# The order of two adaLN tiles on VectorE in the ramp, and a mean taken out by TensorE in the last pieces of a residual block

## The chip, the cores and the metric

One Trainium2 chip, of which one core is used. A core has TensorE (PE in the profile; PEld is its weight loads), VectorE (DVE), ScalarE (ACT), GpSimd (POOL) and SyncE (SP), which issues the loads and stores. TensorE reads on-chip memory and writes only the accumulation banks (PSUM, eight banks of 128x512 fp32 here); VectorE and ScalarE read both, GpSimd only the on-chip memory. The metric is the device time of one execution in microseconds, lower is better.

## The reference

A block of three sublayers over x of 256 x 2048 (fp32), conditioned on a vector c. From c come nine vectors of 2048, `silu(c) @ w_ada + b_ada`: a shift, a scale and a gate for each sublayer.

```python
mod = (jax.nn.silu(c) @ w_ada[l] + b_ada[l]).reshape(B, N_SUBLAYERS, 3, D_MODEL)
shift, scale, gate = mod[:, :, 0], mod[:, :, 1], mod[:, :, 2]

def modulate(h, s):
    return _layer_norm(h) * (1.0 + scale[:, s, None, :]) + shift[:, s, None, :]

y = _swiglu(modulate(x, 0), ffn1_w13[l], ffn1_w2[l])
x = _layer_norm(ALPHA * x + FFN_WEIGHT * gate[:, 0, None, :] * y, ln_g[l, 0], ln_b[l, 0])
...
y = _swiglu(modulate(x, 2), ffn2_w13[l], ffn2_w2[l])
x = _layer_norm(ALPHA * x + FFN_WEIGHT * gate[:, 2, None, :] * y, ln_g[l, 2], ln_b[l, 2])
```

The middle sublayer, left out here, is a mixer of mLSTM heads and a gated recurrence. The change touches the start of the first feed-forward sublayer (FFN1) and the layer norm that ends the last one (FFN2).

## The kernel before, in words

**Numbers.** Products are made of fp32 numbers split in two parts: `hi`, a cast by ScalarE, and `lo`, the rest, by VectorE (`split`, lines 90 to 100). A product then has three matmuls: hi x hi, hi x lo, lo x hi. In a few places both operands stay fp32 and one "whole" matmul does it; the profile shows such a matmul as two records.

**The ramp** (`ramp`, lines 682 to 824) is the start of FFN1. The shift and scale come as adaLN tiles: tile `ada<i>` is 128x2048 weights, and VectorE reduces it against the row of silu(c) (`ada_tile`, line 181) to one column of shift or of scale. Only then can 128 rows of the modulated input u be made, so the ramp goes through the 16 blocks of 128 in stages of 3, 4, 4 and 5 (`STAGES`). In each stage TensorE multiplies the blocks made so far by the weight tiles `rra<n>` (`hra`, `lra` once split), and the partial sums are kept on chip. At the end of a stage (line 781) the u of the next one is made: `ada_until` reduces the adaLN tiles that are still missing, and `modulate` (line 223) lets TensorE transpose two blocks into a bank, ScalarE apply scale and shift to each (line 236) and cast both to the high part (line 239), and VectorE make the low part (line 240). In stage 0 the blocks 3 and 4 are made by a first `modulate` (tile `u0_3`), blocks 5 and 6 by a second (tile `u0_5`). adaLN tiles ada12 and ada13 are the shift and the scale of block 6. The first products of stage 1 are whole ones with the unsplit tile 9 (line 803), the next use tile 10.

**The order.** While `wide[0]` holds, the operations on VectorE and SyncE are recorded through a helper (line 122) that keeps them in program order; all these have L122 in the profile. Elsewhere a scheduler places them. Every engine works off its own queue in order, and the raw tiles live in a few buffers that are used again in turn.

**The end** (`closing`, line 880, and `boundary`, line 330, with `following` None). The output is 2 halves of 128 rows (t = 0, 1) by 4 pieces of 512 columns (n = 0 to 3). Pieces n = 0, 1, 2 get their residual from `residual` (line 309), which also gathers statistics; only n = 3 is left for `boundary`. `products(1)` makes the last product `tl` of rows 128 to 255. `take` adds it to x and gathers statistics, and `norm` aggregates them to mean and variance (`mvp`), lets GpSimd make the reciprocal root `rsp` in two operations, and runs VectorE over the four pieces twice: first (x - mean) * ln_g (line 376), then times rsp plus ln_b (line 386). Each finished piece is stored at once (line 387). x keeps the result in place.

Of the kernel before, what the change touches and what calls it, by code (L numbers as in the profile page):

```python
# [11 lines left out]
F32 = mybir.dt.float32  # L12
# [4 lines left out]
P = 128  # L17
# [30 lines left out]
def block_kernel(ctx: ExitStack, tc: tile.TileContext, a: dict, out: bass.AP):  # L48
# [145 lines left out]
    def ada_until(s, j, kt):  # L194

        while any(key == (s, j, kt) for _, key in todo):
            ada_tile(V if wide[0] else nc.vector)
# [132 lines left out]
    def boundary(s, ps, hls, order, mm, sts, following, gated=False):  # L330
# [19 lines left out]
        def products(t):  # L350
            for n in order[t]:
                if (t, n) not in ps:
                    ps[t, n] = bank(f"tl{s}{t}{n}")
                mm(ps[t, n], t, n)

        def take(t, n):

# [7 lines left out]
            V.bn_stats(sts[t][:, n, :], x[:, t, cs[n]])  # L365
            yield

        def norm(t):

            mv = sm.tile([P, 2], F32, tag="mv", name=f"mvp{s}{t}")  # L370
            V.bn_aggr(mv, sts[t].rearrange("p a b -> p (a b)"))
            r = rstd_in_order(mv[:, 1:2], f"p{s}{t}")

            sq = sums[t] = sm.tile([P, 2, 4], F32, tag="sq", bufs=2, name=f"sq{s}{t}")
            for c in cs:
                V.scalar_tensor_tensor(x[:, t, c], x[:, t, c], mv[:, 0:1], g[:, c], op0=ALU.subtract, op1=ALU.mult)
                yield
            for n, c in enumerate(cs):
                if following:
                    V.scalar_tensor_tensor(x[:, t, c], x[:, t, c], r, b[:, c], op0=ALU.mult, op1=ALU.add,  # L380
                                           accum_out=sq[:, 0, n:n + 1])
                    junk = sm.tile([P, 512], F32, tag="gy" if t else "u", bufs=2, name=f"junk{s}{t}{n}")
                    A.activation(junk, x[:, t, c], AF.Square, bias=sbs, scale=D ** -0.5,
                                 accum_out=sq[:, 1, n:n + 1])
                else:
                    V.scalar_tensor_tensor(x[:, t, c], x[:, t, c], r, b[:, c], op0=ALU.mult, op1=ALU.add)
                    nc.sync.dma_start(out[t * P:(t + 1) * P, c], x[:, t, c])
                yield
            if following:
                tot = tots[t] = sm.tile([P, 4], F32, tag="tot", bufs=2, name=f"tot{s}{t}")  # L390
                V.tensor_reduce(tot[:, 0:2], sq, op=ALU.add, axis=mybir.AxisListType.X)

                V.tensor_scalar(tot[:, 2:3], tot[:, 0:1], 1.0 / D, sb, op0=ALU.mult, op1=ALU.add)
                V.scalar_tensor_tensor(tot[:, 3:4], tot[:, 2:3], tot[:, 2:3], tot[:, 1:2], op0=ALU.mult,
                                       op1=ALU.subtract)
                r = rstd_in_order(tot[:, 3:4], f"n{s}{t}", -1.0)
                nm_ = sm.tile([P, 2], F32, tag="nb", name=f"nbn{s}{t}")
                A.activation(nm_[:, 0:1], tot[:, 2:3], AF.Identity, bias=sb, scale=-1.0)
                A.activation(nm_[:, 1:2], nm_[:, 0:1], AF.Copy, scale=r)
                mrb[t] = nm_[:, 0:1], r, nm_[:, 1:2]  # L400
                yield
# [55 lines left out]
        def takes(t, ns):  # L457
            for n in ns:
                yield from take(t, n)

        def run(steps, m=100):
            for _ in range(m):
                if next(steps, steps) is steps:
                    return

        mrb, sums, tots = {}, {}, {}
        products(0)
        for k in ready:
            fw[k] = split(fw[k], nc.scalar, V)
        run(takes(0, order[0]))  # L470
        products(1)
        if not following:
            run(norm(0))
            run(takes(1, order[1]))
            run(norm(1))
            return

        A.activation(b, b, AF.Identity, accum_out=sb)
# [136 lines left out]
    def ffn(s, w13, w2, start, following=None):  # L615
# [66 lines left out]
        def ramp(ns):  # L682
# [5 lines left out]
            for st, k in enumerate(STAGES):  # L688
# [89 lines left out]
                for b in range(RAMP // 4):  # L778
                    for p in range(2):

                        if b == RAMP // 4 - 1 and p == (k > 2) and not last:
                            k1 = k0 + k
                            tile_of(3 * k - 1)
                            wide[0] = st < len(STAGES) - 2
                            ahead = load(a["w13_r"][n_w + 3 * k], f"ra{n_w + 3 * k}")
                            unsplit = [] if first else None
                            if not first:
                                ahead = split(ahead, nc.scalar, V if wide[0] else nc.vector)
                            ada_until(0, 1, k1 + 1)
                            modulate(0, ns, k1, 2, vec=V if wide[0] else nc.vector, kept=unsplit)  # L790
                            ada_until(0, 1, k1 + STAGES[st + 1] - 1)
                            made = modulate(0, ns, k1 + 2, STAGES[st + 1] - 2, vec=V if wide[0] else nc.vector, kept=unsplit)
                        if (b, p) in held:
                            pss = held[b, p]
                        else:
                            pss = banks(b, p)
                            with ExitStack() as stack:
                                for m in made if b < 2 else ():
                                    stack.enter_context(tc.issue_after(m.ins))
                                if st == 1 and (b, p) == (0, 0):  # L800
                                    for j in range(k):
                                        for t in range(NT):
                                            end = nc.tensor.matmul(
                                                pss[t], unsplit[j][:, t * P:(t + 1) * P],
                                                ahead[0][:, j * 512:(j + 1) * 512], start=j == 0, stop=j == k - 1)
                                else:
                                    end = products(b, p, pss, 0, k)
                                for i in range(k if first else 0, 0 if last else min(3 * k, ((2 * b + p + 3) * k + 3) // 4)):
                                    tile_of(i)
                        if b != KEPT:  # L810
                            for t in range(NT):
                                if first:
                                    A.copy(part[b, p][t], pss[t])
                                else:
                                    (nc.vector if last else V).tensor_add(part[b, p][t], part[b, p][t], pss[t])
                        if first and b < 2 and p:
                            tile_of(4 + b)
                        turn_one(end)
                    if last and b < 4:
                        g, v = (kept if b == KEPT else {p: part[b, p] for p in range(2)}).values()  # L820
                        for t in range(NT):
                            swiglu(b, t, g[t], v[t])
# [57 lines left out]
        def closing(gi):  # L880

            kgs = [(kg, hts[kg // 2], kg % 2 * 4) for kg in (2 * gi - 2, 2 * gi - 1, 2 * gi)]
            pss, hls = {}, {}

            def gated(k, into=None):

                tile = load(w2[kgs[k][0] * 4 + 3], f"w2{s}l{k}", into)
                for c in range(0, D, 512):
                    nc.vector.tensor_mul(tile[0][:, c:c + 512], tile[0][:, c:c + 512], gate[:, 1536:])
                hls[k] = split(tile, nc.scalar, nc.vector)  # L890

            for i, (n, k) in enumerate(((0, 0), (0, 1), (1, 0), (0, 2), (1, 1), (1, 2), (2, 0), (2, 1), (2, 2))):
                kg, h, k0 = kgs[k]
                if not k:
                    pss[n] = [bank(f"tl{s}{t}{n}") for t in range(NT)]
                end = mov_w(pss[n], load_w(w2[kg * 4 + n], f"w2{s}_{kg}_{n}"), *h, k0, not k, k == 2)
                if i:
                    turn_one(end)

                if i in (2, 5):  # L900
                    gated(i // 2, half(i // 5))
                if k == 2:
                    for t in range(NT):
                        residual(s, t, n, pss[n][t], sts, nc.vector)
            credit[:] = 0.0, 0.0
            fine[0] = True
            gated(0)

            def last(ps, t, n):
                for i, (_, h, k0) in enumerate(kgs):  # L910
                    mov_t(ps, hls[i], *h, k0, t, i == 0, i == 2)

            boundary(s, {}, hls, ((3,), (3,)), last, sts, None, True)

# [491 lines left out]
```

## Time and profile before

| | us |
|---|---|
| median of 3 runs | 1898.51 (1898.49 to 1898.91) |
| the profiled execution, its own time | 1898.66 |
| its span, first to last instruction | 1896.9 |
| TensorE busy | 1878.0 |
| VectorE busy | 1412.4 |
| ScalarE busy | 830.8 |
| granted TensorE clock, mean of the span | 0.998 of full |

The page lists the busy time of each engine, the span in 40 slices, the DMA queues, a chain of work followed back from the last instruction, and the costliest groups. Times within the execution are counted from its first instruction. In a row of the timeline stand the start, the length, the engine, the line, the operation, what it writes and reads (buffer numbers left out), its shape, the count, and in brackets the idle time of the engine before it and what ended it. A row of groups ends in count | busy us, mean ns | idle before it and its releasers. A row of waits has the total, the number and the longest.

### The profile page before, as it was taken

Reading aid. Unit: us, or ns where it says so; the run is one execution under the profiler, and the core shown is the slowest. Engines: PE = TensorE matmul, PEld = TensorE weight load, DVE = VectorE, ACT = ScalarE, POOL = GpSimd, SP = SyncE. Lnnn points to the kernel's source line nnn. Section 1 sums busy time; section 2 is a strip of 40 time slices with the busy share of each in tenths; the row PEclk is TensorE's granted clock in tenths of the full one; section 3 lists DMA queues with packets and bytes.
Section 4 is the critical chain, followed back from the end, with each engine's and each line's share of the span. In section 5 each row is a group of like instructions: output and inputs, shape, how many; then the busy total and the mean of one; then the engine's idle time right before and its main releaser. Section 6 shows DMA issues by size and latency. Waiting matters only on the chain.

```text
span 1896.9 us, 21238 instructions
## 1 busy us (share of the span) xinstructions
PE 1878.0 (99%) x8583; PEld 1542.9 (81%) x8583; DVE 1412.4 (74%) x1372; ACT 830.8 (44%) x788; POOL 39.3 (2%) x65
## 2 busy tenths in 40 slices
PE   9999999999999999999999999999999999999997
PEld 6788888888888888788888887888888888888886
DVE  6899998887887977799987877556555644545676
ACT  4443444534334335756643357343434334343340
POOL 0000000000000000000000121000000000000000
PEclk9999999999999999999999999999999999999999
DMA  9989889999999886477787563666666655555562
GB/s 379 404 349 362 321 314 354 353 346 347 353 359 356 333 327 247 174 278 273 275 320 270 218 245 132 242 255 247 241 258 240 230 192 197 182 198 205 195 222 89
DMA packets 74498, 515.87 MB, mean 272 GB/s; under 512 B 8688, under 2 KB 8864, under 8 KB 13472
## 3 DMA queue, kind: packets, MB, share of 16 engines
q1 hardware_dynamic: 72144, 507.54, 71.0%
q10 hardware_dynamic: 1728, 3.80, 0.6%
q0 software_dynamic: 528, 3.17, 0.4%
q8 instruction: 67, 1.10, 0.2%
q14 instruction: 31, 0.25, 0.0%
HBM read 512.36 MB, written 2.12 MB: 271 GB/s over the span
## 4 chain that ended last, share of the span: by engine, by line
PE 93%; DVE 3%; ACT 2%; DMA 1%; issue 1%; POOL 0%; DVEq 0%; SPq 0%; ACTq 0%
PE py L272 6%; PE py L271 6%; PE py L273 6%; PE fg L272 6%; PE fg L271 6%; PE fg L273 6%; PE fv L271 6%; PE fv L272 6%; PE fv L273 6%; PE pj L260 5%; PE pj L262 3%; PE tl L271 2%; PE tl L272 2%; PE tl L273 2%; PE rv L720 2%; PE rv L721 2%
## 5 line engine op out<-in xcount | busy, mean ns | idle before, releaser
L191 DVE CUSTOM_DVE_ANT_0 ada<-ada,scb,badac 128x2048 f32<-128x2048 f32 x110 | 258.0, 2346 | 12.7 <-DMA ada<-in_w_ada 12.6
L99 DVE TENSOR_TENSOR lw<-rw,hw 128x2048 fp32r<-128x2048 f32 x81 | 185.3, 2290 | 92.9 <-ACT hw L97 92.9
L97 ACT CAST hw<-rw 128x2048 fp32r<-128x2048 f32 x81 | 155.0, 1914 | 220.3 <-PE py L273 78.6
L99 DVE TENSOR_TENSOR lfv<-rfv,hfv 128x2048 fp32r<-128x2048 f32 x60 | 137.5, 2292 | 132.5 <-ACT hfv L97 132.4
L99 DVE TENSOR_TENSOR lfg<-rfg,hfg 128x2048 fp32r<-128x2048 f32 x60 | 137.5, 2291 | 90.6 <-ACT hfg L97 90.6
L272 PE MATMUL py<-lw,hth 128*128 128x512 f32 x512 | 199.4, 389 | 0.1
L273 PE MATMUL py<-hw,htl 128*128 128x512 f32 x512 | 199.4, 389 | 0.0
L97 ACT CAST hfg<-rfg 128x2048 fp32r<-128x2048 f32 x60 | 114.9, 1915 | 191.4 <-PE fv L273 57.5
L271 PE MATMUL py<-hw,hth 128*128 128x512 f32 x512 | 197.7, 392 | 0.0
L272 PE MATMUL fg<-lfg,u 128*128 128x512 f32 x480 | 187.0, 389 | 0.1
L273 PE MATMUL fg<-hfg,u 128*128 128x512 f32 x480 | 187.0, 389 | 0.0
L272 PE MATMUL fv<-lfv,u 128*128 128x512 f32 x480 | 186.8, 389 | 0.0
L273 PE MATMUL fv<-hfv,u 128*128 128x512 f32 x480 | 186.7, 389 | 0.0
L97 ACT CAST hfv<-rfv 128x2048 fp32r<-128x2048 f32 x60 | 114.7, 1912 | 164.1 <-PE fg L273 91.7
L271 PE MATMUL fg<-hfg,u 128*128 128x512 f32 x480 | 185.0, 392 | 0.0
L271 PE MATMUL fv<-hfv,u 128*128 128x512 f32 x480 | 183.5, 389 | 0.0
L260 PE MATMUL pj<-u,hs 128*128 128x512 f32 x512 | 122.5, 391 | 0.0
L97 ACT CAST hra<-rra 128x2048 fp32r<-128x2048 f32 x38 | 72.6, 1916 | 102.5 <-DMA rra<-in_w_r 47.7
L272 PEld LDWEIGHTS py<-lw,hth 128*128 128x128 f32 x512 | 96.2, 188 | 20.4 <-DVE lw L99 0.9
L273 PEld LDWEIGHTS py<-hw,htl 128*128 128x128 f32 x512 | 96.1, 188 | 20.2
L271 PEld LDWEIGHTS py<-hw,hth 128*128 128x128 f32 x512 | 95.9, 188 | 19.3
L260 PEld LDWEIGHTS pj<-u,hs 128*128 128x128 f32 x512 | 94.3, 188 | 18.4
(464 smaller groups left out, 3545.9 us busy)
## 6 DMA issues: line engine op xcount, KB each, us to landing
ada<-in_w_ada SPq DMA_DIRECT2D x138, 1024.0 KB, 6.2
rw<-in_w SPq DMA_DIRECT2D x81, 1024.0 KB, 5.0
rfg<-in_w SPq DMA_DIRECT2D x60, 1024.0 KB, 4.9
rfv<-in_w SPq DMA_DIRECT2D x60, 1024.0 KB, 4.8
rra<-in_w_r SPq DMA_DIRECT2D x45, 1024.0 KB, 7.2
rs<-in_w_s SPq DMA_DIRECT2D x32, 1024.0 KB, 5.0
rwo<-in_w_out SPq DMA_DIRECT2D x16, 1024.0 KB, 4.8
rv<-in_w_vo SPq DMA_DIRECT2D x8, 1024.0 KB, 4.8
```

The lines of the kernel that those rows point to most:

```text
L97: act.copy(cut(hi, w), like(raw[:, w], hi))
L99: low.tensor_sub(cut(lo, w), like(raw[:, w], lo), cut(hi, w).bitcast(F32))
L191: vec.tensor_tensor_reduce(raw[:, c], raw[:, c], scb[:, c], 1.0, base, ALU.mult, ALU.add, to)
L260: nc.tensor.matmul(ps, hi[:, k * P:(k + 1) * P], both(k), start=k == 0, stop=False)
L262: nc.tensor.matmul(ps[:, 0:S], lo[:, k * P:(k + 1) * P], uh[:, k, :], start=False, stop=k == KT - 1)
L271: nc.tensor.matmul(o, acth[:, k0 + j, tk], cut(hi, w), start=first and j == 0, stop=False)
L272: nc.tensor.matmul(o, acth[:, k0 + j, tk], cut(lo, w), start=False, stop=False)
L273: end = nc.tensor.matmul(o, actl[:, k0 + j, tk], cut(hi, w), start=False, stop=last and j == 3)
L720: pe.matmul(pss[t], uh[:, k0 + j, tk], hi[:, w], start=go, stop=False)
L721: pe.matmul(pss[t], uh[:, k0 + j, tk], lo[:, w], start=False, stop=False)
```

## The change

Two edits.

In the ramp the second `ada_until` (up to the last block of the next stage) takes the place of the first and comes ahead of the first `modulate`. VectorE's queue at the end of stage 0, as a difference (- before, + now; `ada12` and `ada13` are the reductions of block 6, `u0_3` the low part of blocks 3 and 4, `u0_5` of blocks 5 and 6):

```order
-L122 TENSOR_TENSOR u2_114<-u0_3_505,u2_114 128x2x256
-L122 ISA ada12_510,adac_116<-ada12_510,scb_80,badac_115 128x2048
-L122 ISA adac_116 128x1
-L122 ISA ada13_513,adac_116<-ada13_513,scb_80,badac_115 128x2048
-L122 ISA adac_116 128x1
+L122 ISA ada12_500,adac_116<-ada12_500,scb_80,badac_115 128x2048
+L122 ISA adac_116 128x1
+L122 ISA ada13_503,adac_116<-ada13_503,scb_80,badac_115 128x2048
+L122 ISA adac_116 128x1
+L122 TENSOR_TENSOR u2_114<-u0_3_511,u2_114 128x2x256
 L122 TENSOR_TENSOR u2_114<-u0_5_521,u2_114 128x2x256
```

The low part of `u0_3` moved behind both reductions, next to the low part of `u0_5`. In the ramp nothing else differs: the queues of TensorE, ScalarE and SyncE hold the same instructions in the same order, and at the ends of stages 1 and 2 VectorE's does too, since no adaLN tile is missing there.

At the end, pieces n = 0 and 1 of rows 128 to 255 (`early`) take another way. After their statistics VectorE multiplies them by ln_g; TensorE, behind the last product, copies each into a bank with a whole product by the identity (start) and adds -mean * ln_g to it by a product of ln_g with a diagonal of -mean (stop), which ScalarE makes in two operations. The last pass over these two reads the bank (`tz`). The pieces 2 and 3 go as before, and now first. VectorE's last rows before, from the last product's sum on:

```order
L122 TENSOR_TENSOR x<-x,tl_12778 128x512
L122 BN_STATS sts_8511<-x 128x6
L122 BN_AGGR mvp_12836<-sts_8511 128x2
L122 SCALAR_TENSOR_TENSOR x<-x,mvp_12836,ln_g_12735 128x512 x4
L122 SCALAR_TENSOR_TENSOR x<-x,rsp_12840,ln_b_12737 128x512 x4
```

And VectorE's last rows now:

```order
L122 TENSOR_TENSOR x<-x,tl_12782 128x512
L122 BN_STATS sts_8511<-x 128x6
L122 BN_AGGR mvp_12842<-sts_8511 128x2
L122 SCALAR_TENSOR_TENSOR x<-x,mvp_12842,ln_g_12735 128x512 x2
L122 SCALAR_TENSOR_TENSOR x<-x,rsp_12846,ln_b_12737 128x512 x2
L122 SCALAR_TENSOR_TENSOR x<-tz_12739,rsp_12846,ln_b_12737 128x512
L122 SCALAR_TENSOR_TENSOR x<-tz_12740,rsp_12846,ln_b_12737 128x512
```

Two passes with the mean are gone, and two of the passes with the root read banks. The two products with ln_g stand further ahead on VectorE, between the last split of a weight tile (line 99) and the residual of piece 2 (line 313). TensorE's last rows now, of which the four with `tz` are new (`dm` is the diagonal):

```order
L273 MATMUL tl_12782<-u_114,htl_12382 128x512
L122 MATMUL tz_12739<-x,ident 128x512
L122 MATMUL tz_12740<-x,ident 128x512
L122 MATMUL tz_12739<-ln_g_12735,dm_12851 128x512
L122 MATMUL tz_12740<-ln_g_12735,dm_12851 128x512
```

All four stand behind the last product of the kernel. The diff, cut to what does this:

```diff
@@ products, in boundary
-                mm(ps[t, n], t, n)
+                end = mm(ps[t, n], t, n)
+            return end
@@ norm, in boundary
-        def norm(t):
+        def norm(t, early={}):
...
-            for c in cs:
+            if early:
+                nm_ = sm.tile([P, 2], F32, tag="nb", name=f"nbn{s}{t}")
+                A.mul(nm_[:, 0:1], mv[:, 0:1], -1.0)
+                diag = sm.tile([P, 512], F32, tag="gy", bufs=2, name=f"dm{s}{t}")[:, 0:P]
+                A.activation(diag, ident, AF.Copy, scale=nm_[:, 0:1])
+                for n in early:
+                    T.matmul(early[n], diag, g[:, cs[n]], start=False, stop=True)
+            for n, c in enumerate(cs):
+                if n in early:
+                    continue
                 V.scalar_tensor_tensor(x[:, t, c], x[:, t, c], mv[:, 0:1], g[:, c], op0=ALU.subtract, op1=ALU.mult)
                 yield
-            for n, c in enumerate(cs):
+            for n in sorted(range(4), key=lambda n: n in early):
+                c = cs[n]
...
-                    V.scalar_tensor_tensor(x[:, t, c], x[:, t, c], r, b[:, c], op0=ALU.mult, op1=ALU.add)
+                    V.scalar_tensor_tensor(x[:, t, c], early.get(n, x[:, t, c]), r, b[:, c], op0=ALU.mult, op1=ALU.add)
@@ boundary
+        if not following:
+            early = {n: bank(f"tz{s}{n}") for n in (0, 1)}
+            for n in early:
+                V.tensor_mul(x[:, 1, cs[n]], x[:, 1, cs[n]], g[:, cs[n]])
         products(0)
...
-        products(1)
+        end = products(1)
         if not following:
             run(norm(0))
+            with tc.issue_after(end.ins):
+                for n in early:
+                    T.matmul(early[n], ident, x[:, 1, cs[n]], start=True, stop=False)
             run(takes(1, order[1]))
-            run(norm(1))
+            run(norm(1, early))
             return
@@ ramp
-                            ada_until(0, 1, k1 + 1)
+                            ada_until(0, 1, k1 + STAGES[st + 1] - 1)
                             modulate(0, ns, k1, 2, vec=V if wide[0] else nc.vector, kept=unsplit)
-                            ada_until(0, 1, k1 + STAGES[st + 1] - 1)
                             made = modulate(0, ns, k1 + 2, STAGES[st + 1] - 2, vec=V if wide[0] else nc.vector, kept=unsplit)
```

In `closing`, the function `last` now returns the last matmul, for the order above.

More of the change, by code (lines that the diff above doesn't have):

```diff
@@ L910, in last @@
                 for i, (_, h, k0) in enumerate(kgs):
-                    mov_t(ps, hls[i], *h, k0, t, i == 0, i == 2)
+                    end = mov_t(ps, hls[i], *h, k0, t, i == 0, i == 2)
+                return end
             boundary(s, {}, hls, ((3,), (3,)), last, sts, None, True)
```

## The prediction

> **What bounds the kernel now.** First the page's busy shares and its chain of work that ended last.
>
> ```profile
> PE 1878.0 (99%) x8583; PEld 1542.9 (81%) x8583; DVE 1412.4 (74%) x1372; ACT 830.8 (44%) x788; POOL 39.3 (2%) x65
> PE 93%; DVE 3%; ACT 2%; DMA 1%; issue 1%; POOL 0%; DVEq 0%; SPq 0%; ACTq 0%
> ```
>
> TensorE (PE) is busy for 99% of the span and carries 93% of the chain, so time can be gained only where TensorE stands still, or after its last product. The view of waits, for TensorE alone, says where it stands still; these are the two rows that touch the change.
>
> ```profile
> PE rv L721 <- DVE lra L122: 0.7, 1, 0.7
> PE rg L803 <- ACT u L236: 0.4, 1, 0.4
> ```
>
> Both are one-time waits at the turn from ramp stage 0 to stage 1. The chain of waits from 70 to 84 us (start, length, what) says what they hang on.
>
> ```profile
> 71.94 2.35 DVE ada L122
> 74.29 2.27 DVE ada L122
> 76.60 0.57 ACT u L236
> ...
> 78.79 1.81 ACT hra L97
> 80.62 2.30 DVE lra L122
> 82.97 0.50 PE rv L721
> ```
>
> Two adaLN reductions (ada12, ada13) on VectorE release the last u of the stage, then ScalarE casts it, copies two banks and splits weight tile 10, VectorE makes that tile's low part, and TensorE goes on. The reductions start only at 71.94, and the timeline of VectorE shows why:
>
> ```profile
> 71.33 0.69 DVE L122 TENSOR_TENSOR u<-u,u 128x512 fp32r<-128x512 f32 x1 [3.17 <-ACT u L239]
> ```
>
> VectorE idled 3.17 us for ScalarE's cast of the first u, whose low part stood ahead of the reductions.
>
> At the kernel's end VectorE and GpSimd carry the chain (timeline, closing rows):
>
> ```profile
> 1885.26 0.39 PE L273 MATMUL tl<-u,htl 128*128 128x512 f32 x1
> 1885.69 0.69 DVE L122 TENSOR_TENSOR x<-x,tl 128x512 f32<-128x512 f32 x1 [1.02 <-PE tl L273]
> 1887.14 0.26 DVE L122 BATCH_NORM_AGGREGATE mvp<-sts 128x2 f32<-128x24 f32 x1
> 1887.44 2.74 DVE L122 SCALAR_TENSOR_TENSOR x<-x,mvp,ln_g 128x512 f32<-128x512 f32 x4
> 1887.49 0.75 POOL L122 TENSOR_SCALAR vep<-mvp 128x1 f32<-128x1 f32 x1 [6.38 <-DVE mvp L122]
> 1888.32 0.94 POOL L122 TENSOR_TENSOR rsp<-vep,mhalf 128x1 f32<-128x1 f32 x1
> 1890.10 2.73 DVE L122 SCALAR_TENSOR_TENSOR x<-x,rsp,ln_b 128x512 f32<-128x512 f32 x4
> ```
>
> After the last product come an add, statistics, four passes that take out the mean, four that scale. The scale r is ready at 1889.26, before the mean passes end.
>
> **The change, first part: the ramp.** Nothing is added; one 0.69 us subtraction moves behind two reductions on VectorE. SyncE's issues keep their order, so what counts is whether the reductions' data are in. Of ada12 and ada13 the tile view gives issue times and time to landing:
>
> ```profile
> L122 SPq DMA_DIRECT2D ada<-in_w_ada x2: 327/328/328, 58.2 to 60.9; - x2
> DMA to landing us min/median/max: 10.5/10.7/10.8
> ```
>
> With the longer time for the first issue and the shorter for the second they land at 58.2 + 10.8 = 69.0 and 60.9 + 10.5 = 71.4 (the reverse would make them 68.7 and 71.7). VectorE is free from 71.33 - 3.17 = 68.16, so the first reduction runs from 69.0 to 71.3, and the second waits a moment for its data and runs from about 71.5 to 73.8, where it ended at 76.56. That is 2.7 us earlier, and the chain behind it moves with it: low part of tile 10 done at 82.92 - 2.7 = 80.2. The moved subtraction follows at 73.8 to 74.5, in a stretch where VectorE has no other ready work; its result is first used by tile 10's products.
>
> TensorE does not gain all of that, because it had work. Its rows there:
>
> ```profile
> 74.11 2.74 PE L803 MATMUL rg<-rra,u 128*128 128x512 f32 x6
> 77.22 4.56 PE L803 MATMUL rg<-rra,u 128*128 128x512 f32 x10 [0.37 <-ACT u L236]
> 81.21 1.03 PE L720 MATMUL rv<-hra,u 128*128 128x512 f32 x2
> 82.97 0.50 PE L721 MATMUL rv<-lra,u 128*128 128x512 f32 x1 [0.72 <-DVE lra L122]
> 83.30 0.40 PE L722 MATMUL rv<-hra,u 128*128 128x512 f32 x1
> ```
>
> A record that restarts TensorE is 0.1 longer (0.50 against 0.40 in the last two rows), so the unsplit fp32 records have a pitch of (4.56 - 0.1 - 2.74) / 4 = 0.43 us. The seventh was due at 74.11 + 6 x 0.43 = 76.69 and came at 77.22; with the 0.1 that is 0.63. The second gap: the pair ends at 82.24, its second of 0.40 began at 81.84, the next was due 0.23 later at 82.07 and came at 82.97; with 0.1 again, 1.00. Without both gaps TensorE reaches tile 10's low part at 82.07 - 0.63 = 81.4, when it has been ready for 1.2 us. Gain: **1.63 us**. Bounds: the idle time of the rows alone, 0.37 + 0.72 = 1.1, and the chain's whole 2.7.
>
> Is it kept? Tile 12 is the first whose load is issued by the moved work, and in the trace it lands just as ScalarE starts on it:
>
> ```profile
> 84.17 1.92 ACT L97 CAST hra<-rra 128x2048 fp32r<-128x2048 f32 x1 [1.78 <-DMA rra<-in_w_r]
> 90.76 2.29 DVE L122 TENSOR_TENSOR lra<-rra,hra 128x2048 fp32r<-128x2048 f32 x1
> DVE x L122 <- PE rg L722: 4.1, 2, 2.0
> ```
>
> The queues are full there, so it may land hardly earlier; but its cast ends at 86.1 and VectorE takes it up at 90.76, 4.7 us later, more than the 2.7 by which VectorE moves ahead. Later in that stage VectorE itself waits 4.1 us for TensorE, so from there all engines follow TensorE, 1.63 us early.
>
> **Second part: the end.** Removed: two of four mean passes, each (1890.10 - 1887.44) / 4 = 0.665 us. VectorE is then ready at 1887.44 + 1.33 = 1888.77, before r: the end of the GpSimd row sets the start of the scaling, at 1889.26 + 0.04 = 1889.30 if it still takes 0.94 (0.04 is also the step from the aggregate's end to the pass behind it). Beside lighter VectorE work the second operation was shorter (another boundary):
>
> ```profile
> 762.90 0.55 POOL L122 TENSOR_TENSOR rsn<-ven,mhalf 128x1 f32<-128x1 f32 x1
> ```
>
> With 0.55, r comes at 1888.87 and scaling starts at 1888.91. Against 1890.10 the gain is 0.80 to 1.19; VectorE falls idle halfway through that operation, so I take the middle, **0.95**, a little short of 1.0.
>
> Added on VectorE: two products with ln_g at 0.69 each, ahead of the last but one residual, where it idles 4.23 us, with ln_g landed 1850.3 + 4.5 = 1854.8:
>
> ```profile
> 1866.65 0.69 DVE L313 TENSOR_TENSOR gy<-tl,gate 128x512 f32<-128x512 f32 x1 [4.23 <-PE tl L273]
> L248 SPq DMA_DIRECT2D ln_g<-in_ln_g x1: 328/328/328, 1850.3 to 1850.3; - x1
> DMA to landing us min/median/max: 4.5/4.5/4.5
> ```
>
> Free; without that idle time they would cost 1.4 us. Added on ScalarE and TensorE: a 128x1 negation, a 128x128 scaled identity, four fp32 products. Nearest rows, from the groups by shape and the timeline:
>
> ```profile
> L122 ACT ACTIVATE u<-tu,adac 128x128 f32<-128x128 f32 x24 | 9.0, 458 | 1.0 <-PE tu L122 1.0
> 25.66 1.98 PE L122 MATMUL rg<-rra,u 128*128 128x512 f32 x4 [1.56 <-ACT u L122]
> ```
>
> The second row is four records, which is two such products: 1.72 us at pitch 0.43. The identity pair runs from 1885.5 to 1887.2, beside the add and the statistics. With 0.46 for each ScalarE operation the diagonal is ready at 1887.44 + 0.92 = 1888.4; the second pair then delivers at 1889.4 and 1890.3. VectorE wants these banks at 1889.15 + 1.33 = 1890.5 and, one pass later, 1891.1: slack 0.8. Not on the path.
>
> Scaling from a bank instead of from memory: 689 ns against 692 for the like add, so I charge nothing:
>
> ```profile
> L122 DVE TENSOR_TENSOR x<-x,tl 128x512 f32<-128x512 f32 x2 | 1.4, 689 | 7.0 <-PE tl L273 7.0
> L314 DVE TENSOR_TENSOR x<-x,gy 128x512 f32<-128x512 f32 x2 | 1.4, 692 | 0.1
> ```
>
> [...]
>
> **Sum.** 1.63 + 0.95 = 2.58 us. The profiled execution took 1898.66 (span 1896.9); less 2.58 is 1896.08. The median of the runs is 0.15 below it: **1895.9**, or 0.14% less.
>
> **Rivals.** (a) The ramp's gain is hidden: if the transfers, which cannot come faster, set TensorE's pace in stage 1, only 0.95 is left: 1897.6. For it: ScalarE's wait on tile 12. Against it: the 4.7 us of slack. (b) TensorE later inherits all of VectorE's lead, 2.7, with 0.95 to 1.19 at the end: 1894.9 to 1894.6. Against it: VectorE's 4.1 us wait on TensorE. (c) The new products run at half clock. The mean clock of the last stretch is low:
>
> ```profile
> 1870.00:1897.00 27.00, 15.65 (x70) 12.62 (x68) 15.52 (x25) 0.00 (x0) 3.37 (x4) 0.83 0.23 78
> 24.00:28.00 4.00, 2.44 (x7) 1.14 (x7) 1.86 (x4) 1.01 (x2) 0.00 (x0) 1.00 1.03 409
> ```
>
> If it fell to half, it did so 27 x 0.17 / 0.5 = 9.2 us before the end, at 1887.8, some 2.2 us after the last product. Were all four products at half clock, the pairs would end at 1888.9 and 1892.4 and the last scaling at 1893.3, 0.5 later than now: 1897.4 with the ramp's gain. Against it: a gap of 1.56 us at 25.66 left the clock at 1.00, and here the gap is 1888.4 - 1887.2 = 1.2. [...] (d) Slower: an engine on the closing chain has to fetch instructions there, since the program grew at its end.
>
> ```profile
> q8 instruction: 67, 1.10, 0.2%
> ```
>
> Priced at a landing like ln_g's, 4.5 us, it gives 1900.4; it decides from 2.6 us on. Against it: 67 such fetches passed without showing among TensorE's waits.
>
> **How the numbers follow.** Forecast 0.70, (a) 0.08, (b) 0.14, (c) 0.05, (d) 0.03. The range reaches from (b) to (a): 1894.7 to 1897.6. About 0.2% (3.8 us) is what a measurement of this kernel tells from no change: 1894.7 and below counts as faster, over half of (b), 0.08; slower by that much only the worst of (d), 0.02; the rest 0.90.
>
> **What would show it.** Right: the first reduction starts near 69 and the second ends near 73.8; both TensorE waits are gone from 74 to 84; TensorE then stays 1.6 us early up to 1885; scaling starts near 1889.2 and never waits for TensorE. Wrong: the second reduction waits long for its transfer; new waits of TensorE between 84 and 210; VectorE idle ahead of the last two scalings.

## The result, and the profile after

The changed kernel takes 1895.72 us (median of 22 executions, 1895.04 to 1897.92); before takes 1898.65 us on the same chip (22 executions, 1897.94 to 1900.53). That is 2.93 us or 0.16% less; the ratio is 0.9984, with a 95% interval of 0.9978 to 0.9991. The profiled execution took 1895.58 us with a span of 1893.8 us, at a mean granted clock of 0.999; it is 3.08 us below the profiled execution of before.

The busy shares and the chain of work that ended last, from the page of the changed kernel:

```profile
PE 1880.4 (99%) x8591; PEld 1544.5 (82%) x8591; DVE 1411.9 (75%) x1372; ACT 831.2 (44%) x790; POOL 41.3 (2%) x65
PE 94%; DVE 3%; DMA 1%; ACT 1%; issue 1%; POOL 0%; POOLq 0%; DVEq 0%; SPq 0%; ACTq 0%
```

TensorE has eight records more (two banks, two products each, two records a product) and still sets the time. Its view of waits no longer has the two rows at the turn of stage 0 to stage 1. One row is new, the products that wait for the scaled identity; the other one below stood in before as well:

```profile
PE tz L122 <- ACT dm L122: 0.8, 1, 0.8
PE rv L738 <- ACT u L236: 0.5, 1, 0.5
```

**The ramp.** VectorE's timeline in the changed kernel (start, length, what, idle time before it and what ended that):

```profile
69.25 2.35 DVE L122 CUSTOM_DVE_ANT_0 ada<-ada,scb,badac 128x2048 f32<-128x2048 f32 x1 [0.97 <-DMA ada<-in_w_ada]
71.74 2.35 DVE L122 CUSTOM_DVE_ANT_0 ada<-ada,scb,badac 128x2048 f32<-128x2048 f32 x1
74.01 0.69 DVE L122 TENSOR_TENSOR u<-u,u 128x512 fp32r<-128x512 f32 x1
75.38 0.69 DVE L122 TENSOR_TENSOR u<-u,u 128x512 fp32r<-128x512 f32 x1 [0.68 <-ACT u L239]
78.15 2.29 DVE L122 TENSOR_TENSOR lra<-rra,hra 128x2048 fp32r<-128x2048 f32 x1 [2.08 <-ACT hra L97]
```

The first reduction (ada12) starts when its load is in, the second (ada13) 0.14 us after the end of the first, and the low part of tile 10 starts at 78.15, where before had 80.62: VectorE has a lead of 2.47 us. TensorE in the same stretch:

```profile
74.11 7.03 PE L820 MATMUL rg<-rra,u 128*128 128x512 f32 x16
80.57 1.03 PE L738 MATMUL rv<-hra,u 128*128 128x512 f32 x2
81.43 0.39 PE L739 MATMUL rv<-lra,u 128*128 128x512 f32 x1
81.67 0.40 PE L740 MATMUL rv<-hra,u 128*128 128x512 f32 x1
```

The sixteen unsplit records are one row without a break, and the record that followed the second gap (83.30 in before) starts at 81.67: 1.63 us earlier, the term of the forecast. But at the kernel's end TensorE is earlier by more. The closing rows of the changed kernel, TensorE's last product first:

```profile
1883.00 0.40 PE L273 MATMUL tl<-u,htl 128*128 128x512 f32 x1
1883.43 0.69 DVE L122 TENSOR_TENSOR x<-x,tl 128x512 f32<-128x512 f32 x1 [1.03 <-PE tl L273]
1885.18 1.42 DVE L122 SCALAR_TENSOR_TENSOR x<-x,mvp,ln_g 128x512 f32<-128x512 f32 x2
1885.41 0.40 ACT L122 ACTIVATE dm<-ident,nbn 128x128 f32<-128x128 f32 x1
1885.87 1.99 PE L122 MATMUL tz<-ln_g,dm 128*128 128x512 f32 x4 [0.76 <-ACT dm L122]
1886.07 0.94 POOL L122 TENSOR_TENSOR rsp<-vep,mhalf 128x1 f32<-128x1 f32 x1
1887.04 1.41 DVE L122 SCALAR_TENSOR_TENSOR x<-x,rsp,ln_b 128x512 f32<-128x512 f32 x2 [0.44 <-POOL rsp L122]
1888.37 1.40 DVE L122 SCALAR_TENSOR_TENSOR x<-tz,rsp,ln_b 128x512 f32<-128x512 f32 x2
```

The last product starts 2.26 us earlier than in before (1885.26), so the ramp brought 2.26 and not 1.63. From the last add's start to the end of the last scaling it is 1889.77 - 1883.43 = 6.34 us, where before had 1892.83 - 1885.69 = 7.14: the end brought 0.80. Together 3.06, against 3.08 measured.

**Where the other 0.63 us comes from.** Record by record against before, TensorE is 1.63 us early from 83.30 on and gains 0.13, 0.24 and 0.23 at three places, near 88, 94 and 99.5 us (and 0.04 in all beyond). Each is the first record into a new bank. One such turn in before, from TensorE's timeline:

```profile
93.43 0.39 PE L722 MATMUL rg<-hra,u 128*128 128x512 f32 x1
93.80 0.47 PE L720 MATMUL rv<-hra,u 128*128 128x512 f32 x1
94.11 0.39 PE L721 MATMUL rv<-lra,u 128*128 128x512 f32 x1
```

Two steps take 0.68 us where two at the pitch of 0.23 take 0.46. The weight loads at the three turns are late for no named reason ("issue"), and in VectorE's timeline an add into a partial sum that reads the banks of the stretch before stands beside each:

```profile
88.10 0.19 PEld L720 LDWEIGHTS rg<-hra,u 128*128 128x128 f32 x1 [0.26 <-issue]
93.77 0.19 PEld L720 LDWEIGHTS rv<-hra,u 128*128 128x128 f32 x1 [0.37 <-issue]
99.44 0.19 PEld L720 LDWEIGHTS rg<-hra,u 128*128 128x128 f32 x1 [0.38 <-issue]
```

```profile
87.30 1.28 DVE L122 TENSOR_TENSOR yacc<-yacc,rg 128x512 f32<-128x512 f32 x2
92.97 1.29 DVE L122 TENSOR_TENSOR yacc<-yacc,rv 128x512 f32<-128x512 f32 x2
98.64 1.29 DVE L122 TENSOR_TENSOR yacc<-yacc,rg 128x512 f32<-128x512 f32 x2
```

Each row is two adds; the first of them lasts 0.69 us and so ends at 87.99, 93.66 and 99.33. The late weight loads start 0.11 us behind it each time: TensorE waits for the bank that the add releases. In the changed kernel the first of these adds starts at 84.84, 2.46 us earlier, and the three rows of late weight loads are gone from its timeline. That is an inference from times so far; the experiments test it.

### The profile page after: what moved, and what is told of

Its sections match the earlier page's. It is cut to its first block, busy times and chain, and to the rows that moved or that the text cites. A ratio compares the mean times of both kernels' runs of the same rounds, so it can differ in the third digit from the quotient of the medians.

```text
span 1893.8 us, 21255 instructions
## 1 busy us (share of the span) xinstructions
PE 1880.4 (99%) x8591; PEld 1544.5 (82%) x8591; DVE 1411.9 (75%) x1372; ACT 831.2 (44%) x790; POOL 41.3 (2%) x65
## 4 chain that ended last, share of the span: by engine, by line
PE 94%; DVE 3%; DMA 1%; ACT 1%; issue 1%; POOL 0%; POOLq 0%; DVEq 0%; SPq 0%; ACTq 0%
PE py L272 6%; PE py L271 6%; PE py L273 6%; PE fg L272 6%; PE fg L271 6%; PE fg L273 6%; PE fv L271 6%; PE fv L272 6%; PE fv L273 6%; PE pj L260 5%; PE pj L262 3%; PE tl L271 2%; PE tl L272 2%; PE tl L273 2%; PE rv L738 2%; PE rv L739 2%
```

## The experiments

Each kernel was timed in 11 executions beside the kernel before on the same chip; differences are between medians. The 95% intervals of single ratios reach about 0.0009 to either side (1.7 us), so steps of a few tenths are read in the traces and not in the medians.

**The two edits apart.** The first kernel is before with the ramp's edit alone, the second the changed kernel with that edit undone:

```diff
@@ ramp (first kernel: applied to before; second: taken back)
-                            ada_until(0, 1, k1 + 1)
+                            ada_until(0, 1, k1 + STAGES[st + 1] - 1)
                             modulate(0, ns, k1, 2, ...)
-                            ada_until(0, 1, k1 + STAGES[st + 1] - 1)
```

> The ramp edit alone, the kernel's end as before. Theory (two parts: 1.63 us of gaps of TensorE at tile 10, and another 0.63 that TensorE lost in before at three tile turns, near 88.1, 93.8 and 99.5 us, where it waited for VectorE's adds to release accumulation banks, which VectorE's lead now covers): TensorE is 2.26 us early from 100 us on up to its last product, and the time is 1898.65 - 2.26 = 1896.4 us. Rival (the ramp brings only the 1.63 of the forecast, and the other 0.63 came with the edit at the end, through the program's length or its loads): 1.63 us early from 84 us on, 1897.0 us.

Measured: 1896.53 us against 1898.82, that is 2.29 less. Rows of VectorE, the first add of stage 1 and the last add of the kernel:

```profile
85.24 1.28 DVE L122 TENSOR_TENSOR yacc<-yacc,rg 128x512 f32<-128x512 f32 x2
1883.62 0.69 DVE L122 TENSOR_TENSOR x<-x,tl 128x512 f32<-128x512 f32 x1 [1.02 <-PE tl L273]
```

In this execution the loads came a little later, so the first adds lead before by 87.30 - 85.24 = 2.06 us, and the kernel's last add by 1885.69 - 1883.62 = 2.07. The ramp's edit brings more than 1.63 without the other edit: the rival falls.

> The edit at the kernel's end alone, the ramp as before. Theory: all rows up to the last add stand where they stood in before (add at 1885.7), and from the add's start to the end of the last scaling it is 6.34 us in place of 7.14: 0.80 us less, 1897.85 us. Rival (0.63 us of the ramp's 2.26 belongs to this edit): the add comes 0.63 us earlier than in before, and the time is 1897.2 us.

Measured: 1898.16 us against 1898.82, 0.66 less.

```profile
1886.02 0.69 DVE L122 TENSOR_TENSOR x<-x,tl 128x512 f32<-128x512 f32 x1 [1.03 <-PE tl L273]
1890.96 1.41 DVE L122 SCALAR_TENSOR_TENSOR x<-tz,rsp,ln_b 128x512 f32<-128x512 f32 x2
```

The last add is not earlier than in before but 0.33 us later (TensorE is some 0.3 us late from 65 us on, ahead of the place of the ramp's edit), and from there to the end it is 1892.37 - 1886.02 = 6.35 us: the edit at the end is worth 0.8 and nothing ahead of it. The two edits add up, 2.29 + 0.66 = 2.95 against 2.93 for both, nearer than medians of this spread could promise.

**VectorE held back ahead of the first adds of stage 1.** One or four products whose result nothing uses:

```diff
@@ ramp, behind the low parts of stage 1's first weight tiles
+                        if st == 1 and (b, p) == (0, 0):
+                            spent_ = sm.tile([P, 512], F32, tag="gy", bufs=2, name="spent")
+                            for _ in range(1):    # 4 in the second kernel
+                                V.tensor_mul(spent_, scb[:, 0:512], scb[:, 512:1024])
                         if b != KEPT:
```

> The changed kernel with one product of 128x512 more on VectorE, its result used by nothing, right ahead of the first two adds of stage 1 (the adds that release the first banks of that stage); no load and no low part of a weight tile comes later until then. A product between two others takes VectorE 0.6 us there. Theory (TensorE's 2.26 us are 1.63 from the gaps at tile 10 and 0.63 from banks that VectorE's adds release sooner; VectorE's lead over before is 2.47 us, so 0.21 of it is spare): VectorE's lead falls to 1.87, TensorE waits again at the turns near 88 to 100 us and keeps 1.87 us in place of 2.26: 0.4 us lost, 1896.1 us. Rival (the 0.63 does not come from VectorE's adds): TensorE stays 2.26 us early, 1895.7 us.

Measured: 1896.52 us against 1898.61, 2.09 less, so by the medians 0.84 us of the change's gain is lost. VectorE's adds, then the weight load at the turn and the last add:

```profile
86.14 1.27 DVE L122 TENSOR_TENSOR yacc<-yacc,rg 128x512 f32<-128x512 f32 x2
86.93 0.19 PEld L738 LDWEIGHTS rg<-hra,u 128*128 128x128 f32 x1 [0.72 <-ACT hra L97]
1884.52 0.69 DVE L122 TENSOR_TENSOR x<-x,tl 128x512 f32<-128x512 f32 x1 [1.03 <-PE tl L273]
```

The late weight load is back, and again 0.11 us behind the end of the first add (86.14 + 0.68 = 86.82), though the view puts it down to ScalarE. The adds lead before by 1.16 us, the last add by 1.17. In this execution the loss is 2.26 - 1.17 = 1.09 us, more than the 0.4 expected, because its loads were later too: the low part of tile 10 started at 78.85, a lead of 1.77 that the product cut by 0.6. The two later turns show the same: weight loads at 92.60 and 98.27 us, 0.11 us behind the end of the first add of each turn.

> As the run with one more product, with four (2.4 us of VectorE's time) in that place. Theory: VectorE's lead over before falls to 2.47 - 2.4 = 0.07 us, and so does what TensorE keeps: it is 1.6 us early at 84 us and loses it at the turns near 88, 94 and 99.5 us; with the 0.80 at the end the time is 1898.65 - 0.07 - 0.80 = 1897.8 us. Rival (TensorE's lead is its own, and VectorE has the slack of its later 4.1 us wait to give): TensorE keeps 1.63 to 2.26 us, 1895.7 to 1896.4 us.

Measured: 1898.87 us against 1898.61, 1.07 us above the expectation.

```profile
85.12 2.86 DVE L122 TENSOR_TENSOR spent<-scb 128x512 f32<-128x512 f32 x4
87.90 1.28 DVE L122 TENSOR_TENSOR yacc<-yacc,rg 128x512 f32<-128x512 f32 x2
88.70 0.19 PEld L738 LDWEIGHTS rg<-hra,u 128*128 128x128 f32 x1 [2.52 <-issue]
88.73 0.47 PE L738 MATMUL rg<-hra,u 128*128 128x512 f32 x1 [2.13 <-DVE yacc L122]
1886.66 0.69 DVE L122 TENSOR_TENSOR x<-x,tl 128x512 f32<-128x512 f32 x1 [1.03 <-PE tl L273]
```

Now the wait is long enough for the view to name it: TensorE stood 2.13 us for the add. VectorE's lead ahead of the products was 2.18 us (the low part of tile 10 started at 78.44), and the four took 2.78 us, not 2.4, so the adds came 0.60 us later than in before. TensorE lost its 1.63 at once, was 0.60 us late, and lost 0.37 more further on (part of it in a wait of 0.3 us for VectorE between 100 and 210 us): the last add is 0.97 later. So without VectorE's early adds TensorE keeps nothing of the ramp's gain, not even the 1.63.

The executions of all these kernels, those further below too, can be set side by side. TensorE's lead is that of the same matmul in both traces:

| kernel | first adds of stage 1, lead over before, us | TensorE's lead at 75 us, ahead of the two gaps | at 105 us | last add, lead over before, us |
|---|---|---|---|---|
| one piece on TensorE | 2.94 | 0.46 | 2.72 | 2.68 |
| variance + epsilon on ScalarE, ahead of the negation | 2.66 | 0.07 | 2.34 | 2.00 |
| three pieces on TensorE | 2.48 | -0.09 | 2.18 | 2.23 |
| changed | 2.46 | 0.00 | 2.27 | 2.26 |
| variance + epsilon on VectorE | 2.37 | -0.08 | 2.19 | 2.16 |
| ramp's edit alone | 2.06 | 0.07 | 2.06 | 2.07 |
| variance + epsilon on VectorE, three pieces | 2.06 | -0.07 | 2.09 | 2.01 |
| variance + epsilon on ScalarE, behind the negation | 1.57 | -0.26 | 1.61 | 0.90 |
| changed, run again | 1.50 | -0.32 | 1.50 | 1.49 |
| one product more | 1.16 | -0.03 | 1.19 | 1.17 |
| variance + epsilon on VectorE, run again | 0.58 | -1.67 | 0.55 | 0.17 |
| four products more | -0.60 | 0.01 | -0.60 | -0.97 |

At 105 us TensorE's lead is, within 0.04 us in all twelve, the smaller of two numbers: VectorE's lead at the first adds, or its own lead at 75 us plus the 2.27 us that it lost between there and 105 us in before (1.63 in the two gaps, 0.64 at and behind the three turns). Behind 105 us most executions keep their lead; four lose 0.3 to 0.7 us of it. In that with variance + epsilon on ScalarE behind the negation a weight tile landed late: ScalarE's cast waited 5.8 us for it up to 419.74 us, and TensorE lost 0.6 us near 425 us. For the run again of variance + epsilon on VectorE (between 353 and 425 us) and for ScalarE ahead of the negation (near 609 us) the cause was not traced.

**The end: what sets the start of the scaling.** One piece on TensorE in place of two:

```diff
@@ boundary
-            early = {n: bank(f"tz{s}{n}") for n in (0, 1)}
+            early = {n: bank(f"tz{s}{n}") for n in (0,)}    # (0, 1, 2) in the kernel after this
```

> The changed kernel with one piece of the last four taken over by TensorE in place of two: three mean passes stay on VectorE. Theory (the scale r, from GpSimd 1.87 us after the aggregate, sets when scaling starts, and the second removed pass hardly counted): passes end 1885.18 + 3 x 0.67 = 1887.2, r is in at 1887.0, so scaling starts 0.15 us later than in the changed kernel: 1895.9 us. Rival (VectorE's passes are the bound and each counts in full): 0.67 us later, 1896.4 us.

Measured: 1895.90 us against 1898.82. From the last add (1883.01) to the end (1888.74 + 0.75) it is 6.48 us against 6.34: 0.14 more, as expected of a bound by r; the second removed pass was worth 0.14, the first 0.66.

> The changed kernel with three of the last four pieces taken over by TensorE in place of two: one mean pass stays, so VectorE is idle from 1885.9 us on, before GpSimd starts on the power. Theory (GpSimd's second operation takes 0.94 us beside VectorE's passes and 0.55 us beside an idle VectorE): it takes 0.55 here, r is in at 1886.6 and scaling starts 0.4 us sooner than in the changed kernel; the third bank of TensorE, near 1888.9, holds up the last scaling, so the time is 1895.6 us. Rival (the 0.94 has another cause than VectorE's passes): the operation takes 0.94 again, scaling starts where it does in the changed kernel, 1895.75 us. The length of that operation tells the two apart, not the time.

Measured: 1895.38 us against 1898.61. The last mean pass, GpSimd's second operation and the scaling:

```profile
1885.20 0.75 DVE L122 SCALAR_TENSOR_TENSOR x<-x,mvp,ln_g 128x512 f32<-128x512 f32 x1
1886.09 0.55 POOL L122 TENSOR_TENSOR rsp<-vep,mhalf 128x1 f32<-128x1 f32 x1
1886.67 0.75 DVE L122 SCALAR_TENSOR_TENSOR x<-x,rsp,ln_b 128x512 f32<-128x512 f32 x1 [0.72 <-POOL rsp L122]
1887.34 2.18 DVE L122 SCALAR_TENSOR_TENSOR x<-tz,rsp,ln_b 128x512 f32<-128x512 f32 x3
```

With VectorE idle from 1885.95 us on the operation takes 0.55 us, and scaling starts 3.21 us behind the last add's start (1883.46) where the changed kernel needs 3.61. The third bank held up VectorE by 0.1 us or so; it is 6.06 us from add to end.

**The first of GpSimd's two operations elsewhere.**

```diff
@@ norm, for the last token tile
-            r = rstd_in_order(mv[:, 1:2], f"p{s}{t}")
+            V.tensor_scalar(v, mv[:, 1:2], 1.0, EPS, op0=ALU.mult, op1=ALU.add)   # two kernels: on VectorE
+            A.activation(v, mv[:, 1:2], AF.Copy, bias=EPS)   # two kernels: on ScalarE, ahead of A.mul or behind it
+            G.tensor_tensor(r, v, mhalf, op=ALU.pow)
```

> The changed kernel with the first of the two operations that make r, variance + epsilon, on VectorE right behind the aggregate; GpSimd does the power alone. Theory (GpSimd's two operations one behind the other set when scaling starts): the power runs 1885.3 to 1886.25, the two mean passes end near 1886.65 and are now the bound, scaling starts 0.35 us earlier than in the changed kernel: 1895.35 us. Rival (GpSimd is held up as long as VectorE's passes run, whatever it has to do): the power ends near 1887.0 as before and the time stays 1895.7 us.

Measured: 1895.22 us against 1898.82.

```profile
1885.28 0.15 DVE L122 TENSOR_SCALAR vep<-mvp 128x1 f32<-128x1 f32 x1
1885.35 1.41 DVE L122 SCALAR_TENSOR_TENSOR x<-x,mvp,ln_g 128x512 f32<-128x512 f32 x2
1885.51 0.99 POOL L122 TENSOR_TENSOR rsp<-vep,mhalf 128x1 f32<-128x1 f32 x1 [6.56 <-DVE vep L122]
1886.66 1.41 DVE L122 SCALAR_TENSOR_TENSOR x<-x,rsp,ln_b 128x512 f32<-128x512 f32 x2
```

The power now ends at 1886.50, ahead of the passes; scaling follows them without a wait, and from add (1883.53) to end it is 5.87 us, 0.47 less than in the changed kernel. GpSimd was not held for as long as passes ran.

> The changed kernel as it is, beside the two below on one chip, so that they can be compared with it directly: 2.9 us below before, some 1895.7 us.

Measured: 1895.71 us against 1898.81. Its profiled execution was one of the longer ones, 1896.38, and shows one reason why executions differ: its first reduction in the ramp started at 70.21, 0.96 us later than in the profile above. From 10 to 72 us the views of waits of that profile and of this one have:

```profile
ACT hra L122 <- DMA rra<-in_w_r: 12.5, 6, 3.8
```

```profile
ACT hra L122 <- DMA rra<-in_w_r: 13.6, 6, 4.5
```

ScalarE waited 1.1 us longer for the first weight tiles. The last add came 0.77 later (1884.20), less than the 0.96 because VectorE had been 0.2 us ahead of TensorE, and from it to the end it was again 6.34 us.

> The run with variance + epsilon on VectorE, beside the changed kernel on one chip. Its trace had 5.87 us from the last add's start to the end of the last scaling, against 6.34 in the changed kernel. Theory: it is 0.47 us faster than the changed kernel, 1895.25 us. Rival (the two runs lay on different chips or differed by the landing of loads alone): no difference between them.

Measured: 1895.41 us against 1895.71 of the changed kernel. The sign is that of the theory, but 0.3 us is inside the spread of either; only the trace, once more 5.87 us from add to end, carries it.

> As the run with variance + epsilon on VectorE, with three of the last four pieces taken over by TensorE: one mean pass, 0.7 us long, runs beside the first half of GpSimd's power. Theory (an operation of GpSimd that starts beside a pass of VectorE keeps the long duration, as it did in the changed kernel where VectorE fell idle halfway): the power takes 0.95 us again. Rival (it is slowed only as long as VectorE is busy): some 0.75 us. The time: the third bank of TensorE comes 2.85 us behind the diagonal, which holds up the last scaling; 6.05 us from the last add to the end against 5.87, so 1895.4 us, and no faster than with two pieces.

Measured: 1895.31 us against 1898.81.

```profile
1885.50 0.74 DVE L122 SCALAR_TENSOR_TENSOR x<-x,mvp,ln_g 128x512 f32<-128x512 f32 x1
1885.66 0.99 POOL L122 TENSOR_TENSOR rsp<-vep,mhalf 128x1 f32<-128x1 f32 x1 [6.56 <-DVE vep L122]
```

It is the long duration, as the theory said, with VectorE idle from 1886.24 on. From add (1883.68) to end it is 6.08 us, no better than two pieces. But the ends of the operation have a pattern: here it ends 1886.65 - 1886.24 = 0.41 us behind the pass that ran when it started. In the changed kernel the second pass ran from 1885.85 to 1886.60 and the operation ended at 1887.01: 0.41 again. The last two kernels shift its start to see whether that holds.

> The changed kernel with variance + epsilon on ScalarE ahead of the negation; VectorE keeps its two mean passes, GpSimd does the power alone. Times in the frame of the changed kernel's trace (first pass 1885.18 to 1885.93, second 1885.85 to 1886.60): the power starts near 1885.45. Theory (GpSimd's operation waits for the end of the VectorE pass that runs when it starts, and ends 0.41 us behind that end, as in all the traces so far): it ends near 1886.34 and shows some 0.9 us. Rival (it is slower by a fixed amount beside passes: 0.94 to 0.99 us): it ends at 1886.4. Either way the passes, not r, set the start of the scaling at 1886.64, 0.4 us sooner than in the changed kernel: 1895.3 us.

Measured: 1895.38 us against 1898.70; the passes and the power:

```profile
1885.44 1.41 DVE L122 SCALAR_TENSOR_TENSOR x<-x,mvp,ln_g 128x512 f32<-128x512 f32 x2
1885.72 0.88 POOL L122 TENSOR_TENSOR rsp<-vep,mhalf 128x1 f32<-128x1 f32 x1 [6.61 <-ACT vep L122]
```

> As the run before, with variance + epsilon on ScalarE behind the negation, 0.24 us later: the power starts near 1885.67, still beside the first pass. Theory: it ends where it ended in the run before, 0.41 us behind the first pass, near 1886.34, and shows some 0.67 us. Rival (fixed 0.94 to 0.99 us): it ends near 1886.63, 0.24 later than in the run before. The time is the same for both, 1895.3 us; the power's length and end tell.

Measured: 1895.41 us against 1898.70; the first pass and the power:

```profile
1886.54 0.75 DVE L122 SCALAR_TENSOR_TENSOR x<-x,mvp,ln_g 128x512 f32<-128x512 f32 x1
1886.91 0.79 POOL L122 TENSOR_TENSOR rsp<-vep,mhalf 128x1 f32<-128x1 f32 x1 [6.70 <-ACT vep L122]
```

The first pass ends 0.75 us after its start, at 1886.19 and 1887.29, the power at 1886.60 and 1887.70: 0.41 behind it both times. Its start moved by 0.09 us against the pass (0.28, then 0.37; less than the 0.24 expected, since ScalarE began its second operation 0.11 us behind the first) and its length shrank by 0.09. A fixed slowdown is ruled out: in the kernels so far the start within the pass and the length add up to 1.15 or 1.16 us each time (0.16 + 0.99, 0.22 + 0.94, 0.28 + 0.88, 0.37 + 0.79). With variance + epsilon on ScalarE, ahead of the negation, it is 5.80 us from add (1883.69) to end: the shortest end of all, 0.54 less than in the changed kernel. Of these five variants (three pieces; variance + epsilon on VectorE with two or three; on ScalarE) each has a shorter end than the changed kernel in its trace; their medians (3.2 to 3.6 us below before, against 2.9 and 3.1) lean the same way and don't settle the order among them.

## Why the prediction was right, point by point

- **The loads of ada12 and ada13** were forecast to land at 69.0 and 71.4; the reductions started at 69.25 and 71.74 and the second ended near 74.0 in place of 73.8. VectorE's lead came out as 2.47 us, not 2.7. Right.
- **The two gaps of TensorE**, 0.63 and 1.00: both gone, 1.63 to the hundredth.
- **"From there all engines follow TensorE, 1.63 us early"** is the step that failed. It rested on the view of waits, which names no wait of TensorE from 84 to 140 us. The three halts at the turns stood under the weight loads, as "issue". Rival (b), in which TensorE inherits VectorE's lead, held in part: 2.26 of 2.47, until TensorE itself was the limit (2.27). The argument against it, VectorE's 4.1 us wait for TensorE, was of a place further on (135 and 138 us); up to 100 us VectorE paced TensorE through the banks.
- **Rival (a)**, the transfers as the limit: the DMA engines' mean busy share in before was 0.97 from 70 to 84 us and 0.95 from 80 to 90 us, but the slack of tile 12 held (its cast ended at 85.93, VectorE took it up at 88.30), and no new wait of TensorE for a weight tile appeared.
- **The end**: r was the bound, as forecast (one piece less costs 0.14, not 0.67). The size was off: 0.80, not 0.95. The step was the shorter GpSimd operation: taking the middle because VectorE falls idle halfway had no ground. The operation ended 0.41 us behind the pass that ran when it started, and 0.55 us is what it takes with no such pass under way. The row at 762.90 us, from which the 0.55 came, ran beside a statistics operation (762.81 us, 0.69 us long) and was no longer than the 0.55 us with VectorE idle (three pieces); it was no measure for an operation beside these passes, where it took 0.79 to 0.99 us.
- **Free work**: the two products with ln_g were hidden (VectorE's idle time ahead of the residual fell from 4.23 to 2.63 us). The diagonal was ready earlier than forecast, some 0.7 us after the aggregate, the products ended ahead of their use, and VectorE never waited for a bank. Scaling from a bank took 1.40 us for two passes against 1.41 from memory: no cost, as forecast.
- **Rival (c)**, half clock: the two pairs of products took 1.88 and 1.99 us, against 1.98 for the like row at 25.66 us, and the clock fell only behind them (mean granted clock 1.00 from 1880 to 1888 us, 0.87 from 1888 to 1892). In before it was 1.00 from 1886 to 1888 us and 0.51 from 1888 to 1892 (0.54 in the first half microsecond of it), so there it fell some 2.4 us after the last product's end (1885.65), not the 2.2 of the prediction. **Rival (d)**, an instruction fetch: no such halt in the closing rows.

In the profiled execution the time came to 1895.58 against 1896.08 forecast: 0.63 more from the ramp, 0.15 less at the end. The medians are nearer, 1895.7 against 1895.9, and part of that is luck: the forecast put the median 0.15 below the profiled execution, and that of the changed kernel lies 0.14 above, so 0.29 of the error cancelled. The run of the same kernel again shows one execution whose ramp loads were later than in the profiled one; that this is what moves the median was not shown.

## What to carry to other kernels

Before saying that the engine on the path keeps only its own gaps, look at its weight loads too: a short halt at the first record into a new bank, labelled "issue" or put down to another engine, can be a wait for the engine that empties banks, and shows as a constant distance (here 0.11 us) between the two. Where a tiny GpSimd operation sits between VectorE passes like these, count from the end of the pass that runs when it starts (here the power ended 0.40 to 0.41 us behind it), and give the steps ahead of it to an engine that is idle. Gains of half a microsecond in two thousand are read in the trace, between two fixed rows, not in medians.

## What the runs showed of the hardware that was not expected

GpSimd's 128x1 power beside VectorE's passes `x<-x,mvp,ln_g` took 0.79, 0.88, 0.94 or 0.99 us, depending on when within a pass it started (0.37, 0.28, 0.22 or 0.16 us behind the pass's start), and 0.55 with none under way; in the changed kernel and the four with variance + epsilon moved it ended 0.40 to 0.41 us behind that pass (with it on VectorE and two pieces: 1886.50 against 1885.35 + 0.75). The profile's spans of GpSimd are rough, but the scaling that waits for r agrees: in the changed kernel it starts at 1887.04, 0.03 us behind the end shown.

Other rows show the same. Variance + epsilon on GpSimd took 0.75 us beside a pass and ended 0.05 us behind it (1885.23 + 0.75 against 1885.18 + 0.75), and 0.19 us with none under way (781.15 us of before). Two powers in a row, from 1077.08 us of the changed kernel, took 3.10 us and ended 0.41 us behind a subtraction of 128x2048 that ran from 1077.48 to 1079.77 us; in before the same two, with that subtraction starting late in the second (1079.74 us), took 1.08 us. One row does not fit: at 12.39 us of before a power took 0.57 us beside a reduction of 128x1024 that had begun 0.02 us earlier and ran 1.29 us.

The passes lost nothing to it: two of them took 1.41 or 1.42 us with it and 1.41 behind it. In the kernel with variance + epsilon on VectorE the second of them started while the power ran (1885.51 to 1886.50 us), and the two took 1.41 us. Why GpSimd's operation ends a fixed time behind the pass was not shown.
